# Grouping sixteen rounded and sixteen low matmuls in a Trainium2 encoder block, with aligned operands and later residual loads

## The chip, the cores and the metric

The kernel runs on one core of one Trainium2 chip. The core has a matrix engine (TensorE, in the profile PE for its matmuls and PEld for its weight loads), a vector engine (VectorE, DVE), a scalar engine (ScalarE, ACT), a general engine (GpSimd, POOL) and a synchronizing engine (SyncE, SP) that here issues nearly all transfers. The engines run at the same time, each through its own queue in order, and wait for one another by semaphores. The metric is the time of one execution in microseconds (us) of the device; less is better.

## The reference

One encoder layer on 256 tokens of width 2048, in float32:

```python
h = rms_norm(x, attn_norm[i])
proj = h @ w_in[i]
qa, ka, va, qb, kb, vb, ga, gb = jnp.split(proj, split_points, axis=-1)
ya = windowed_gqa(qa, ka, va, rel_bias_table, sink_a[i])
yb = dilated_attention(qb, kb, vb, rel_bias_table)
merged = jax.nn.sigmoid(ga) * (ya @ w_branch_a[i]) + jax.nn.sigmoid(gb) * (yb @ w_branch_b[i])
x = x + merged @ w_out[i]
hf = rms_norm(x, ffn_norm[i])
g = dwconv_centred(hf @ w_ffn_gate[i], conv_w[i], conv_b[i])
x = x + (jax.nn.gelu(g) * (hf @ w_ffn_up[i])) @ w_ffn_down[i]
gate_p = jax.nn.sigmoid(rms_norm(x, ple_norm[i]) @ w_ple_gate[i])
x = x + gate_p * (p[i] @ w_ple_proj[i])
return rms_norm(x, final_norm)
```

There are 8 heads of windowed attention and 12 of dilated attention in three groups, and the MLP is 5632 wide. Nearly all the time goes into the products with the weight matrices.

## The kernel before

**Rounded and low parts.** Products run in a rounded float format (FR in the code). To keep float32 accuracy each operand is split in two: a rounded part, made by ScalarE, and a low part, the rest, made by VectorE as the difference. Three products of parts make one product of the wanted accuracy: rounded by rounded, rounded by low and low by rounded.

**Weights.** All weights come from HBM as 258 pieces of 1 MB, in the order of their use. `load` (L238) has SyncE fetch a piece into one of three raw tiles. `produce` (L244) splits one unit, usually half a piece, 128 x 1024: ScalarE rounds it (L261, `uh`), VectorE takes the difference (L262, `ul`). There are six buffers for each of `uh` and `ul`, and two more of each, `vh` and `vl`, for units made of sums of weights (L254 to L256), in stages that save one product of eight by a Strassen-like scheme. `drop` (L279) gives a unit's buffers back and `pump` (L267) makes the next units at once, as far as buffers are free.

**Two kinds of stage.** In a feature-major stage the weights stand still in the array and the activations move: a block (`block`, L284) multiplies one 128 x 128 piece of weights by one 128-feature slice of the activations. Its first matmul (L289) takes the rounded weights and 512 columns, which are the 256 tokens' rounded and low parts side by side; its second (L290) takes the low weights and the rounded 256 columns, and adds to the second half of the same accumulator. `product` (L295) runs sixteen blocks for the 2048 features of one 128-wide result. The attention's queries and keys (activations `hs`) and the MLP's gate and up projections (activations `hf`) are made so: 544 and 1408 blocks. In the MLP's first half, stage E0, the first four products run jointly, feature slice by feature slice (L952 to L956); E1 is the second half. The first seven products of the attention run jointly too, in a loop of their own at the start (L517 to L529). In a token-major stage the activations stand still and 512 columns of weights move, in threes (`thirds`, L321, lines L324 to L326): gates, branch projections, output projection (D0 and D1), the MLP's way down (F00 to F11) and the last gate. Value products (L302, lines L312 to L314) are of that kind with 256 columns.

**What hangs between blocks.** Work on the side is put down by `at` for a stage, a feature slice and a place, and `run_due` runs it when the loop comes by: the scores of a head (L581 to L583 and L600) at slice 9 of the product after its query, the transposes of the exponentials (L635) at slice 11 or 12 of the next, the product with the values (again L581 to L583) at slice 4 of the one after that. At the MLP's start the last transposes of the activations (`rows_pair`, L812) are put down for slices 2 to 5. A scheduler then sets the final order on each engine, so that rows can move a little from where the code has them; `keep` (L400) pins an instruction to the program's order.

**Residual rows.** The input's rows, to which the output projection adds, are loaded in four transfers of 512 KB into `xr` (`load_rows`, L869), put down for pieces 3 to 6 of stage D0. `xr` takes the place of `ya`, the windowed attention's result, and can't land before its last reader is done.

**Memory.** Tiles stand in pools. Up to the pools of weights and of large activations every tile starts at 160 modulo 512 bytes. The pool `sc` of small tiles has an uneven size, and behind it the attention's tiles and later the token stages' tiles (`vh`, `vl`, sums of activations `S`, a third part of the MLP's activations `act2`) start at 352 modulo 512.

Of the kernel before, what the change touches and what calls it, by code (L numbers as in the profile page):

```python
# [10 lines left out]
F32 = mybir.dt.float32  # L11
# [5 lines left out]
P = 128  # L17
T = 256
D = 2048
KC = D // P  # L20
# [7 lines left out]
NH = QH + BH  # L28
# [57 lines left out]
START = FIRST + 1  # L86
WARM = 9
JOINT = 4
WIDE = 2 * T
_JOBS = _plan()  # L90
NA = len(_JOBS)
# [94 lines left out]
def _encoder(ctx: ExitStack, tc, xt, pt, xrow, cols, gainrow, table, onehot, mask, ident_in, wts, out):  # L186
# [97 lines left out]
    def block(acc, m, first, last):  # L284
# [7 lines left out]
        if o == _LAST_OF[u]:  # L292
            drop(u)

    def product(i, moving, n, ring):  # L295
        acc = bank(ring)
        for k in range(n):
            run_due(i, k)
            block(acc, moving(k), k == 0, k == n - 1)
        return acc  # L300

    def value_product(i, paired):  # L302
# [178 lines left out]
    hs = big.tile([P, KC, 2 * T], FR, name="hs", tag="R0")  # L481
    tot = ap_.tile([P, T], F32, name="tot", bufs=1)
    oh = ap_.tile([NBUCK, 2 * T], F32, name="oh", tag="near", bufs=1)
    tb = sc.tile([NBUCK, NH], F32, name="tb", bufs=1)
    mk = ap_.tile([NH, 2 * T], F32, name="mk", tag="s1", bufs=2)

    order = [(0, 1), (0, 0, 3), (0, 3, 7), (1, 2), (0, 7, 11), (0, 11, PIECE), (2, 3)]
    chunk = 3
# [96 lines left out]
    def scores(heads, y):  # L585

        n = len(heads)
        wide = T if n == 1 else 2 * T
        s = ap_.tile([P, 2, wide], F32, name="s", tag="s%d" % n, bufs=2 if n == 1 else 1)
        h, k = heads[0]  # L590
        sp = bank("sp", P, 2, T)
        for t in range(2):
            thrice(sp[:, t, :], [qs[h][:, c + t * P:c + (t + 1) * P] for c in (0, T)], [ks[k][:, :T], ks[k][:, T:]])
        a, step = (hba[:, h, :], P) if n == 1 else (hbb[:, h - QH, :], 1)
        nc.vector.tensor_tensor(s[:, :, :T], sp, view(a, 0, (step, 2), (1, T)), op=ALU.add)
        if n > 1:
            sp = bank("sp", P, 2, T)
            for g, (h, k) in enumerate(heads[1:]):
                for t in range(2):
                    nc.tensor.matmul(sp[:, t, g * P:(g + 1) * P], qs[h][:, t * P:(t + 1) * P],  # L600
                                     ks[k][:, (1 - t) * P:(2 - t) * P], start=True, stop=True)
# [12 lines left out]
        for t in range(2):  # L614
            nc.scalar.activation(s[:, t, :], s[:, t, :], AF.Exp, bias=nm[:, t:t + 1], accum_out=den[:, t:t + 1])
        if n == 1:
            es = ap_.tile([P, 2], F32, name="es")
            nc.scalar.activation(es, nm, AF.Exp, bias=sk)
            nc.vector.tensor_tensor(den, den, es, op=ALU.add)
        rd = ap_.tile([P, 2], F32, name="rd")  # L620
        nc.vector.reciprocal(rd, den)
        for t in range(2):
            nc.vector.tensor_scalar(s[:, t, :], s[:, t, :], rd[:, t:t + 1], None, op0=ALU.mult)
        return s
# [203 lines left out]
            at(when, merged_pair, "P22", 2 * j + i, c)  # L828

    def halved(r):  # L830
        h = sc.tile([P, 2], F32, name="rh")
        nc.vector.tensor_scalar(h, r[:, :2], 0.5, None, op0=ALU.mult)
        return h

# [32 lines left out]
    xr = big.tile([P, 2, D], F32, name="xr", tag="ya")  # L867

    def load_rows(n):  # L869
        nc.sync.dma_start(xr[:, :, cut[n]], xrow[:, :, cut[n]])  # L870

    def residual(stage, s, moving, key, square):

# [14 lines left out]
        turn_back(which, pair, dst, lambda t: xr[:, t, pair * T:(pair + 1) * T], scale)  # L888

    def rows_root():  # L890
        q = sc.tile([P, 2], F32, name="rs")
        nc.vector.tensor_tensor(q, held["ssq"][:, 0], held["ssq"][:, 1], op=ALU.add)
        return root(q, 2)

    for n in range(4):
        at(("D0", 3 + n, 0), load_rows, n)
    at(("D0", 2, 4), combine, "merged", held["merged"], 6, 2)
    held["ssq"] = sc.tile([P, 2, 2], F32, name="ssq")
    residual("D0", 0, lambda k: held["merged"][:, k, :], "merged", True)
    hf = big.tile([P, KC, 2 * T], FR, name="hf", tag="R0")  # L900
    for pair, when in enumerate((("D1", 0, 2), ("D1", 0, 5), ("D1", 1, 0), ("D1", 1, 3))):
# [43 lines left out]
    for half in range(2):  # L945
# [4 lines left out]
        joint = 0 if half else JOINT  # L950
        stage = "E%d" % half
        accs = [bank(which) for which in ("M1", "M5", "M6", "M7")[:joint]]  # L952
        for k in range(KC if joint else 0):
            run_due(stage, k)
            for a in accs:
                block(a, hf[:, k, :], k == 0, k == KC - 1)  # L956
        for (kind, n), a in zip(jobs, accs):
            mlp(kind, n, a)
        turns["e"] = 0
# [2 lines left out]
        if half:  # L962
# [6 lines left out]
            held["ssq"] = sc.tile([P, 2, 2], F32, name="ssq")  # L969
# [143 lines left out]
```

## Time and profile before

| | |
|---|---|
| median of 3 runs | 1474.07 us (1472.39 to 1474.58) |
| the profiled execution | 1474.83 us, of which the span of the trace is 1473.0 |
| granted TensorE clock | 0.998 |
| VectorE busy | 84% of the span |
| ScalarE busy | 55% of the span |
| moved by DMA | 282.93 MB, mean 192 GB/s |

The prediction shows the lines that carry it. A row of a group reads: line of the code, engine, operation, out<-in by the names of the tiles, shapes, count; then busy time in us and the mean of one in ns; then the engine's idle time before them and who ended it. Durations of matmuls include their way through the array and overlap with the next, so that the pace of a run of matmuls is the difference of two starts, divided by the number of steps between them. A row of the timeline begins with its start in us from the span's start and its duration.

### The profile page before, as it was taken

To read this page: it belongs to the slowest core of one execution; us is meant where nothing else is said; L and a number is where in the kernel's file an instruction comes from. 1 tells how busy PE (TensorE), PEld (TensorE's weight loads), DVE (VectorE), ACT (ScalarE), POOL (GpSimd) and SP (SyncE) were. 2 spreads that over 40 slices of the span, in tenths; PEclk is the share of its full clock that TensorE was granted. 3 is DMA by queue.
4 is the path that set the end of the run, shared out by engine and by line. 5 is a ranking of instruction groups with operands and counts; after the bars stand their busy time and mean duration, and the time that the engine had idled before them with its cause. 6 is when DMAs were issued, how large, how long until landed. Compare 5 with 4: busy or idle time off the path is not lost.

```text
span 1473.0 us, 20121 instructions
## 1 busy us (share of the span) xinstructions
PE 1456.9 (99%) x7766; PEld 1247.8 (85%) x7766; DVE 1241.5 (84%) x1841; ACT 810.5 (55%) x1153; POOL 4.8 (0%) x9
## 2 busy tenths in 40 slices
PE   9999999999999999999999999999999999999997
PEld 8899999988888887888888888888888888888785
DVE  7587665669989989989888899988888889999994
ACT  7466444446555555565555556454555555555763
POOL 0000000000000000000000000000000000000000
PEclk9999999999999999999999999999999999999999
DMA  9654454445456456464555545465545455446462
GB/s 318 236 199 144 154 184 178 160 155 200 172 200 229 169 211 248 155 234 185 199 183 189 201 152 219 181 248 176 196 176 196 178 194 179 184 188 232 168 222 93
DMA packets 46460, 282.93 MB, mean 192 GB/s; under 512 B 5076, under 2 KB 9812, under 8 KB 14108
## 3 DMA queue, kind: packets, MB, share of 16 engines
q1 hardware_dynamic: 45356, 280.20, 52.1%
q10 hardware_dynamic: 1008, 1.45, 0.3%
q8 instruction: 61, 1.00, 0.3%
q14 instruction: 35, 0.29, 0.1%
HBM read 279.49 MB, written 2.14 MB: 191 GB/s over the span
## 4 chain that ended last, share of the span: by engine, by line
PE 91%; DVE 4%; DMA 2%; ACT 1%; issue 1%; POOL 0%; POOLq 0%; ACTq 0%
PE bank L289 31%; PE bank L290 15%; PE bank L324 12%; PE bank L325 12%; PE bank L326 12%; DMA raw<-in_wts 2%; PE bank L312 2%; PE bank L313 2%; PE bank L314 2%; DVE ul L262 1%; DVE vl L262 1%; ACT uh L261 1%; PE bank L812 1%; PE bank L635 0%; PE bank L582 0%
## 5 line engine op out<-in xcount | busy, mean ns | idle before, releaser
L261 ACT ACTIVATE uh<-raw 128x1024 fp32r<-128x1024 f32 (+2 forms) x518 | 522.6, 1017 | 493.1 <-PE bank L289 272.0
L262 DVE TENSOR_TENSOR ul<-raw,uh 128x1024 fp32r<-128x1024 f32 (+2 forms) x518 | 601.0, 1171 | 184.4 <-ACT uh L261 181.8
L289 PE MATMUL bank<-hf,uh 128*128 128x512 f32 x1408 | 493.6, 397 | 0.0
L290 PE MATMUL bank<-hf,ul 128*128 128x256 f32 x1408 | 393.4, 280 | 0.0
L289 PEld LDWEIGHTS bank<-hf,uh 128*128 128x128 f32 x1408 | 264.6, 188 | 63.1
L290 PEld LDWEIGHTS bank<-hf,ul 128*128 128x128 f32 x1408 | 265.7, 189 | 0.2
L289 PE MATMUL bank<-hs,uh 128*128 128x512 f32 x544 | 195.9, 402 | 2.1 <-DVE hs L422 2.1
L290 PE MATMUL bank<-hs,ul 128*128 128x256 f32 x544 | 153.5, 283 | 0.0
L261 ACT ACTIVATE vh<-raw 128x1024 fp32r<-128x1024 f32 x92 | 97.4, 1058 | 59.9 <-DVE raw L254 28.3
L289 PEld LDWEIGHTS bank<-hs,uh 128*128 128x128 f32 x544 | 103.5, 190 | 25.0 <-DVE hs L422 2.4
L262 DVE TENSOR_TENSOR vl<-raw,vh 128x1024 fp32r<-128x1024 f32 x92 | 112.2, 1221 | 0.5 <-ACT vh L261 0.2
L290 PEld LDWEIGHTS bank<-hs,ul 128*128 128x128 f32 x544 | 104.3, 192 | 0.1
L324 PE MATMUL bank<-uh,act 128*128 128x512 f32 x232 | 90.8, 391 | 0.0
L325 PE MATMUL bank<-ul,act 128*128 128x512 f32 x232 | 90.7, 391 | 0.0
L326 PE MATMUL bank<-uh,act 128*128 128x512 f32 x232 | 90.7, 391 | 0.0
L324 PE MATMUL bank<-uh,hs 128*128 128x512 f32 x172 | 67.6, 393 | 0.0
L326 PE MATMUL bank<-uh,hs 128*128 128x512 f32 x172 | 67.5, 392 | 0.0
L325 PE MATMUL bank<-ul,hs 128*128 128x512 f32 x172 | 67.3, 391 | 0.0
L312 PE MATMUL bank<-uh,hs 128*128 128x256 f32 x224 | 63.8, 285 | 0.0
L313 PE MATMUL bank<-ul,hs 128*128 128x256 f32 x224 | 63.5, 283 | 0.0
L314 PE MATMUL bank<-uh,hs 128*128 128x256 f32 x224 | 63.4, 283 | 0.0
L254 DVE TENSOR_TENSOR raw<-raw 128x1024 f32<-128x1024 f32 x46 | 56.2, 1222 | 0.5
(236 smaller groups left out, 2232.4 us busy)
## 6 DMA issues: line engine op xcount, KB each, us to landing
raw<-in_wts SPq DMA_DIRECT2D x251, 1024.0 KB, 4.8
raw<-in_wts SPq DMA_DIRECT2D x12, 512.0 KB, 6.7
xr<-in_xrow SPq DMA_DIRECT2D x4, 512.0 KB, 9.8
x<-in_xt SPq DMA_DIRECT2D x13, 128.0 KB, 5.8
hb<-hold SPq DMA_DIRECT2D x3, 514.0 KB, 7.6
hb<-hold SPq DMA_DIRECT2D x2, 768.0 KB, 6.6
last<-in_gainrow SPq DMA_DIRECT2D x1, 1024.0 KB, 4.8
out<-xr SPq DMA_DIRECT2D x4, 256.0 KB, 2.6
```

Of the source, the lines that this page charges most:

```text
L254: nc.vector.tensor_tensor(raw[:, :2 * WIDE], raw[:, WIDE:3 * WIDE], raw[:, :2 * WIDE], op=ALU.subtract)
L261: nc.scalar.activation(hi, src, AF.Copy)
L262: nc.vector.tensor_tensor(lo, src, hi.bitcast(F32), op=ALU.subtract)
L289: nc.tensor.matmul(acc, hi[:, w], m, start=first, stop=False, skip_group_check=True)
L290: nc.tensor.matmul(acc[:, T:], lo[:, w], m[:, :T], start=False, stop=last, skip_group_check=True)
L312: nc.tensor.matmul(acc[:, :T], xh, hi, start=(k == 0), stop=False)
L313: nc.tensor.matmul(acc[:, :T], xh, lo, start=False, stop=False)
L314: nc.tensor.matmul(acc[:, :T], xl, hi, start=False, stop=(k == KC - 1))
L324: nc.tensor.matmul(acc, sh, wh, start=first, stop=False)
L325: nc.tensor.matmul(acc, sh, wl, start=False, stop=False)
L326: nc.tensor.matmul(acc, sl, wh, start=False, stop=last)
L812: nc.tensor.transpose(p[:, k, t * P:(t + 1) * P], src(t)[:, k * P:(k + 1) * P], ident)
```

## The change

Three edits, and what they move.

**Grouping.** `products` and `unit_blocks` take the place of the loops over `block` in `product` and in E0's joint part. Two units, sixteen blocks, are taken together: first the sixteen matmuls with rounded weights, and then the sixteen with low weights. Work that is due between blocks runs while the rounded matmuls are written out. Both units are given back during the low ones. The joint loop of the first seven products still uses `block`.

**Addresses.** `tb` moves from `sc` to the attention's pool, in the ring of the keys; `rh`, `rs` and `ssq` get one buffer each; the reciprocal's tile `rd` becomes 32 columns wide, of which two are used. By this the attention's tiles and the token stages' `vh`, `vl`, `S` and `act2` start at 160 modulo 512 bytes.

**Residual rows.** `load_rows` is pinned to the program's order.

```diff
+JOINED = 2
...
+    def unit_blocks(todo):
+
+        ends, units = [], []
+        for _ in range(JOINED):
+            u = _FBLOCKS[state["at"] + len(ends)][0]
+            units.append(u)
+            for o in range(_LAST_OF[u] + 1):
+                acc, m, first, last = next(todo)
+                nc.tensor.matmul(acc, weights(u)[0][:, o * P:(o + 1) * P], m,
+                                 start=first, stop=False, skip_group_check=True)
+                ends.append((acc, m, last, u, o))
+        for acc, m, last, u, o in ends:
+            nc.tensor.matmul(acc[:, T:], weights(u)[1][:, o * P:(o + 1) * P], m[:, :T],
+                             start=False, stop=last, skip_group_check=True)
+            if o == _LAST_OF[u]:
+                drop(u)
+        state["at"] += len(ends)
+
+    def products(i, moving, n, accs):
+
+        def todo():
+            for k in range(n):
+                run_due(i, k)
+                for acc in accs:
+                    yield acc, moving(k), k == 0, k == n - 1
+
+        blocks, end = todo(), state["at"] + n * len(accs)
+        while state["at"] < end:
+            unit_blocks(blocks)
...
     def product(i, moving, n, ring):
         acc = bank(ring)
-        for k in range(n):
-            run_due(i, k)
-            block(acc, moving(k), k == 0, k == n - 1)
+        products(i, moving, n, [acc])
         return acc
...
-    tb = sc.tile([NBUCK, NH], F32, name="tb", bufs=1)
+    tb = ap_.tile([NBUCK, NH], F32, name="tb", tag="k", bufs=7)
...
-        rd = ap_.tile([P, 2], F32, name="rd")
-        nc.vector.reciprocal(rd, den)
+        rd = ap_.tile([P, 32], F32, name="rd")
+        nc.vector.reciprocal(rd[:, :2], den)
...
-        h = sc.tile([P, 2], F32, name="rh")
+        h = sc.tile([P, 2], F32, name="rh", bufs=1)
...
-        nc.sync.dma_start(xr[:, :, cut[n]], xrow[:, :, cut[n]])
+        keep(nc.sync.dma_start(xr[:, :, cut[n]], xrow[:, :, cut[n]]))
...
-        for k in range(KC if joint else 0):
-            run_due(stage, k)
-            for a in accs:
-                block(a, hf[:, k, :], k == 0, k == KC - 1)
+        if joint:
+            products(stage, lambda k: hf[:, k, :], KC, accs)
```

On TensorE, in the product that holds the sums of squares for the first norm (`tot` by `ones`) and the spread of its root (`rdg`), blocks alternated before:

```order
L290 MATMUL bank<-hs,ul 128x256
L289 MATMUL bank<-hs,uh 128x512
L290 MATMUL bank<-hs,ul 128x256
L429 MATMUL bank<-ones,tot 128x1 x4
L289 MATMUL bank<-hs,uh 128x512
L290 MATMUL bank<-hs,ul 128x256
```

Now the same product and the first score matmul (`kf` by `qf`) of the next stand so:

```order
L304 MATMUL bank<-hs,uh 128x512 x6
L459 MATMUL bank<-ones,tot 128x1 x4
L304 MATMUL bank<-hs,uh 128x512 x8
L480 MATMUL bank<-rdg,ones 128x256
L304 MATMUL bank<-hs,uh 128x512 x2
L308 MATMUL bank<-hs,ul 128x256 x16
L304 MATMUL bank<-hs,uh 128x512 x9
L611 MATMUL bank<-kf,qf 128x256
```

The sixteen low matmuls have moved behind all rounded ones, and side work has only rounded matmuls of its own product ahead of it. In the MLP 86 of the 88 rounded groups stand as one row of sixteen.

On VectorE, around the last query (`q`) of a group of dilated heads and the eviction of its scores (`s`), before:

```order
L262 TENSOR_TENSOR ul<-raw,uh 128x1024
L411 SCALAR_TENSOR_TENSOR u<-bank,t 128x256
L659 TENSOR_TENSOR ya<-bank,ya 128x256
L712 TENSOR_TENSOR q<-u,rms 128x128x2
L262 TENSOR_TENSOR ul<-raw,uh 128x1024 x2
L411 SCALAR_TENSOR_TENSOR u<-bank,t 128x256
L712 TENSOR_TENSOR q<-u,rms 128x128x2
L262 TENSOR_TENSOR ul<-raw,uh 128x1024
L595 TENSOR_TENSOR s<-bank,hb 128x2x256
```

and now:

```order
L263 TENSOR_TENSOR ul<-raw,uh 128x1024 x2
L441 SCALAR_TENSOR_TENSOR u<-bank,t 128x256
L742 TENSOR_TENSOR q<-u,rms 128x128x2
L689 TENSOR_TENSOR ya<-bank,ya 128x256
L263 TENSOR_TENSOR ul<-raw,uh 128x1024 x2
L441 SCALAR_TENSOR_TENSOR u<-bank,t 128x256
L742 TENSOR_TENSOR q<-u,rms 128x128x2
L625 TENSOR_TENSOR s<-bank,hb 128x2x256
```

The low units now come in twos between the products' evictions, and the unit that stood between the query and the scores' eviction is among those ahead of the query.

On SyncE, around the loads of the residual rows (`xr`), before:

```order
L241 DMA raw<-in_wts 128x2048 x78
L870 DMA xr<-in_xrow 128x2x512 x2
L241 DMA raw<-in_wts 128x2048 x2
L870 DMA xr<-in_xrow 128x2x512 x2
L241 DMA raw<-in_wts 128x2048 x143
```

and now:

```order
L242 DMA raw<-in_wts 128x2048 x83
L900 DMA xr<-in_xrow 128x2x512
L242 DMA raw<-in_wts 128x2048
L900 DMA xr<-in_xrow 128x2x512
L242 DMA raw<-in_wts 128x2048
L900 DMA xr<-in_xrow 128x2x512
L242 DMA raw<-in_wts 128x2048
L900 DMA xr<-in_xrow 128x2x512
L242 DMA raw<-in_wts 128x2048 x137
```

The first load stands five raw tiles later than before, and one raw tile stands between each two of the four.

More of the change, by code (lines that the diff above doesn't have):

```diff
@@ L293, in block @@
             drop(u)
+    def unit_blocks(todo):
[23 more added lines that the diff above has]
+            unit_blocks(blocks)
+        assert next(blocks, None) is None
     def product(i, moving, n, ring):
         acc = bank(ring)
-        for k in range(n):
-            run_due(i, k)
-            block(acc, moving(k), k == 0, k == n - 1)
+        products(i, moving, n, [acc])
         return acc
@@ L890, in rows_root @@
     def rows_root():
-        q = sc.tile([P, 2], F32, name="rs")
+        q = sc.tile([P, 2], F32, name="rs", bufs=1)
         nc.vector.tensor_tensor(q, held["ssq"][:, 0], held["ssq"][:, 1], op=ALU.add)
@@ L897, in _encoder @@
     at(("D0", 2, 4), combine, "merged", held["merged"], 6, 2)
-    held["ssq"] = sc.tile([P, 2, 2], F32, name="ssq")
+    held["ssq"] = sc.tile([P, 2, 2], F32, name="ssq", bufs=1)
     residual("D0", 0, lambda k: held["merged"][:, k, :], "merged", True)
@@ L968, in _encoder @@
                 nc.vector.tensor_tensor(pl_[k], pr[:, k], ph_[k].bitcast(F32), op=ALU.subtract)
-            held["ssq"] = sc.tile([P, 2, 2], F32, name="ssq")
+            held["ssq"] = sc.tile([P, 2, 2], F32, name="ssq", bufs=1)
         residual("F%d0" % half, 0, activation_row, "act", half)
```

## The prediction

> **What bounds the kernel now.** I read the busy shares first, then the groups of instructions, the engine's own waits, and last the timeline of single matmuls, because the first view alone says only "TensorE".
>
> ```profile
> span 1473.0 us, 20121 instructions
> PE 1456.9 (99%) x7766; PEld 1247.8 (85%) x7766; DVE 1241.5 (84%) x1841; ACT 810.5 (55%) x1153; POOL 4.8 (0%) x9
> PE 91%; DVE 4%; DMA 2%; ACT 1%; issue 1%; POOL 0%; POOLq 0%; ACTq 0%
> ...
> PE bank L582 <- DVE qf L417: 0.7, 1, 0.7
> ```
>
> TensorE is busy for 99% of the span, it carries 91% of the chain that ended last, and its own list of waits, of which one is shown, holds six entries, none above 2.1 us. So nothing but the pace of the matmuls, and those few waits, can move the time much. Busy time doesn't tell the pace, since matmuls overlap: it has to be taken from start to start. The timeline of TensorE gives it (columns: start, duration, engine, line, operation). In the first half of the MLP, then in its second half:
>
> ```profile
> 699.85 0.28 PE L290 MATMUL bank<-hf,ul 128*128 128x256 f32 x1
> ...
> 710.94 0.28 PE L290 MATMUL bank<-hf,ul 128*128 128x256 f32 x1
> ```
>
> ```profile
> 1050.03 0.28 PE L290 MATMUL bank<-hf,ul 128*128 128x256 f32 x1
> ...
> 1060.99 0.28 PE L290 MATMUL bank<-hf,ul 128*128 128x256 f32 x1
> ```
>
> The first pair of rows spans 32 blocks (a block is one L289 and one L290): 11.09 / 32 = 346.6 ns each. The second spans 31: 10.96 / 31 = 353.5 ns. Nothing waits in either stretch; the same alternation simply settles into a fast or a slow beat. Two places show what a run of equal matmuls takes:
>
> ```profile
> 479.62 0.39 PE L325 MATMUL bank<-ul,ya 128*128 128x512 f32 x1
> ...
> 487.78 0.39 PE L325 MATMUL bank<-ul,yb 128*128 128x512 f32 x1
> ```
>
> ```profile
> 923.64 0.39 PE L326 MATMUL bank<-uh,act 128*128 128x512 f32 x1
> ...
> 936.88 0.39 PE L324 MATMUL bank<-uh,act 128*128 128x512 f32 x1
> ```
>
> ```profile
> 50.78 0.28 PE L314 MATMUL bank<-uh,hs 128*128 128x256 f32 x1
> ...
> 57.98 0.28 PE L314 MATMUL bank<-uh,hs 128*128 128x256 f32 x1
> ```
>
> 512 columns after 512 columns: 8.16 / 36 = 226.7 ns in the branch projections, and 13.24 / 58 = 228.3 ns in the down projection, where VectorE and ScalarE work harder. 256 after 256, in a value product: 7.20 / 60 = 120.0 ns. A rounded and a low matmul, each among its like, would thus take 346.7 to 348.3 ns: the fast beat, and never the slow one.
>
> **The change part by part.** The sum is made against the profiled execution, 1474.83 us (a span of 1473.0 and 1.8 around it), which is 0.76 above the median of 1474.07.
>
> *Grouping.* No instruction is added or removed; of 1952 blocks the 112 of the start stay alternating, and 1840 are grouped: 704 in each half of the MLP and 432 in the attention projections. I take 347.5 ns, the middle of 346.7 and 348.3. The second half gains 704 x (353.5 - 347.5) = 4.2 us, the first loses 704 x 0.9 = 0.6. For the attention projections the trace has this stretch and these means:
>
> ```profile
> 187.80 0.28 PE L290 MATMUL bank<-hs,ul 128*128 128x256 f32 x1
> ...
> 196.98 0.28 PE L290 MATMUL bank<-hs,ul 128*128 128x256 f32 x1
> ```
>
> ```profile
> L289 PE MATMUL bank<-hs,uh 128*128 128x512 f32 x526 | 187.1, 398 | 0.0
> L290 PE MATMUL bank<-hs,ul 128*128 128x256 f32 x528 | 147.9, 281 | 0.0
> L289 PE MATMUL bank<-hf,uh 128*128 128x512 f32 x1408 | 493.6, 397 | 0.0
> L290 PE MATMUL bank<-hf,ul 128*128 128x256 f32 x1408 | 393.4, 280 | 0.0
> ```
>
> 9.18 / 26 = 353.1 ns, the slow beat. The MLP's means of 397 and 280 ns come from one half fast and one slow; those of the attention projections are 1 ns higher each, so I put two thirds of their blocks in the slow beat: 288 x 5.6 - 144 x 0.9 = 1.5 us. Together -5.1 us; -6.5 at 346.7 ns and -3.6 at 348.3.
>
> By the Trainium skill, "TensorE: Matmul & The Clock Gate", section "Back-to-back issue gap", a warm matmul of N columns follows its predecessor after N / 2.4 + 2.5 ns, which is 215.8 and 109.2 here and 325 for a block in whatever order. The trace doesn't agree (346.6 and 353.5, against 226.7 and 120.0 in runs), and it is the difference between the orders that the term above uses.
>
> *What the grouping moves.* Six pairs of weight buffers feed TensorE. Two are now in hand at once, and the next pair of units is wanted two groups later, 2 x 16 x 0.3475 = 11.1 us, while making a unit takes this:
>
> ```profile
> L262 DVE TENSOR_TENSOR ul<-raw,uh 128x1024 fp32r<-128x1024 f32 x468 | 568.0, 1222 | 166.9 <-ACT uh L261 164.4 <-PE bank L289 1.6
> ```
>
> 2 x 1.22 = 2.4 us of VectorE, behind ScalarE's 1.06 each (the first row below): hidden. But work that hangs between blocks is reached sooner, since only rounded matmuls stand before it: at the tenth block by 9 x 125 ns = 1.1 us. The tightest such place is the score matmul that follows the last query of a head group:
>
> ```profile
> 152.36 1.06 ACT L261 ACTIVATE uh<-raw 128x1024 fp32r<-128x1024 f32 x1 [1.71 <-PE bank L289]
> 153.46 1.23 DVE L262 TENSOR_TENSOR ul<-raw,uh 128x1024 fp32r<-128x1024 f32 x1 [1.55 <-ACT uh L261]
> 155.05 0.64 DVE L712 TENSOR_TENSOR q<-u,rms 128x256 f32<-128x256 f32 x1
> 156.11 1.05 PE L600 MATMUL bank<-k,q 128*128 128x128 f32 x8
> ```
>
> The query is ready at 155.69, TensorE wants it at 156.11. TensorE arrives 1.1 us earlier, but the query does too, by about 1 us: ScalarE waited here for the product's last rounded matmul, which now stands 16 x 0.12 = 1.9 us before the product's end, so the rounded weights are made before the eviction instead of ahead of it. VectorE then makes two low units before the query, as the order shows. Two of the four such places lie in grouped products; with the chain at the first head (the 0.7 us wait above) and the transposes that start the MLP I allow +0.5 us, between 0 and 3 x 1.1 = 3.3.
>
> *Residual rows.* SyncE issued two of these loads at 545.03, behind a wait for the last reader of their buffer, and ahead of two raw tiles:
>
> ```profile
> 545.03 1.31 SPq L870 DMA_DIRECT2D xr<-in_xrow  x2
> 547.96 1.47 SPq L241 DMA_DIRECT2D raw<-in_wts  x2
> 547.96 7.46 DMA raw<-in_wts
> raw<-in_wts SPq DMA_DIRECT2D x251, 1024.0 KB, 4.8
> 555.52 1.06 ACT L261 ACTIVATE uh<-raw 128x1024 fp32r<-128x1024 f32 x1 [3.92 <-DMA raw<-in_wts]
> 558.76 0.39 PE L325 MATMUL bank<-ul,merged 128*128 128x512 f32 x1
> 560.83 0.66 PE L812 MATMUL bank<-ident,c 128*128 128x128 f32 x4 [1.69 <-DVE merged L816]
> ```
>
> The raw tile took 7.46 us where the median is 4.8, ScalarE stood for it, VectorE's queue slid, and TensorE lost 2.07 - 0.23 = 1.84 us at the transposes. Issued at the same 547.96 and landing in 4.8 it would be there 2.7 us sooner, more than the stall: -1.8 us (bounds 0 and -1.8). What is late next? The first load now goes five raw tiles later, some 5 x 4.8 = 24 us, near 569; with the median landing of 9.8 us it is there at 579, and its reader starts at 594:
>
> ```profile
> xr<-in_xrow SPq DMA_DIRECT2D x4, 512.0 KB, 9.8
> L878 DVE TENSOR_TENSOR xr<-xr,bank x4: 678/683/687, 594.3 to 600.2; 128x512 f32<-128x512 f32 x4
> ```
>
> *Residues.* The pools move, so that the token-stage tiles lose their offset of 352 and stand at 160 modulo 512, as the others do. Where operands of both kinds meet, matmuls are a little longer:
>
> ```profile
> L324 PE MATMUL bank<-uh,act 128*128 128x512 f32 x232 | 90.8, 391 | 0.0
> L324 PE MATMUL bank<-uh,S 128*128 128x512 f32 x46 | 18.3, 399 | 0.0
> L325 PE MATMUL bank<-ul,S 128*128 128x512 f32 x46 | 18.2, 396 | 0.0
> L326 PE MATMUL bank<-uh,S 128*128 128x512 f32 x46 | 18.1, 393 | 0.0
> L325 PE MATMUL bank<-vl,act 128*128 128x512 f32 x20 | 8.0, 401 | 0.0
> L324 PE MATMUL bank<-vh,S 128*128 128x512 f32 x138 | 54.5, 400 | 0.0
> ```
>
> Against 391: 46 x (8 + 5 + 2) = 0.7 us, and some 60 matmuls at 10 ns, 0.6. The 138 at 400 have both operands at 352 and wait for VectorE at times; at 9 ns they hold 1.2 more. Bounds 0 and -2.5; I take -1.5, near the 1.3 of the mixed rows. The other edits (single buffers, a wider reciprocal tile) move addresses alone and cost nothing.
>
> By the Trainium skill, "SBUF — State Buffer", section "Who interferes with whom", "PE and ACT never wait on anyone", so addresses should not matter. The rows of 399 and 401 ns lean the other way, though they differ in more than the residue.
>
> **Sum.** -5.1 - 1.8 - 1.5 + 0.5 = -7.9 us: 1466.9 for the profiled execution, and **1466.2** beside the median of 1474.07.
>
> **Rivals.** *Residues give nothing* (the rows differ because of waits): 1467.7. That is also the time by the SBUF page's rule.
>
> *The slow beat survives grouping*, or the order doesn't matter: for it speaks that the same code holds both beats, against it that no long run of equal matmuls shows the slow one. Without the first term: 1471.3. The TensorE page's formula would give this too.
>
> *Early arrival ends slower.* Twelve heads have scores and transposes between blocks, and four transposes start the MLP. If TensorE waits the full 1.1 us at each of 16 places, that costs 17.6, less 8.4 saved: 1483.3. It turns the sign from the eighth place on. Against it: one wait of 0.7 us is all that TensorE's list shows there today.
>
> *The change doesn't do what it says*: the scheduler could split the groups. The order shows 86 of the MLP's 88 rounded groups whole, so no chance of its own.
>
> **How the numbers follow.** The forecast 0.42, residues nothing 0.25, slow beat 0.18, early arrival 0.08, better than every bound 0.07. With all bounds at their best the sum is -10.8, which is 1463.3; with all at their worst -0.3, 1473.8. The range 1462.0 to 1473.8 takes in the first three cases and leaves out most of the last two, 0.15. A change of 0.2%, 2.9 us, is about what a measurement of this kernel can tell from none: faster (below 1471.1) 0.42 + 0.25 + 0.07 and a third of the slow-beat case, less 0.02 for a forecast with its terms at their worst, 0.78; within it 0.14; slower 0.08.
>
> **What would show it.** Start to start, 512-column matmuls of the second half at 226.7 to 228.3 ns and 256-column ones at 120; both halves of the MLP equally long; no wait before L812 near 560; the rows of S at 391. Wrong would be: rounded groups above 233 ns, new waits of TensorE for q, s or xr, a first reader of the residual rows that waits for a DMA.

## The result and the profile after

| | before | after |
|---|---|---|
| median of 6 runs each | 1473.09 us | 1466.06 us (1464.90 to 1467.14) |
| ratio, 95% interval | | 0.9951 (0.9938 to 0.9963) |
| the profiled execution, and its span | 1474.83 us, 1473.0 | 1467.14 us, 1465.3 |

The time is 0.14 us from the forecast of 1466.2. This is partly luck. The forecast started from 1474.07 us; beside the change the kernel before took 1473.09, so by the medians the gain is 7.0 us where 7.9 were forecast. And the profile shows two terms that were wrong by almost 2 us each, in opposite directions.

Busy shares and the chain that ended last, from the page of the kernel after:

```profile
span 1465.3 us, 20083 instructions
...
PE 1450.7 (99%) x7766; PEld 1250.4 (85%) x7766; DVE 1248.0 (85%) x1841; ACT 826.2 (56%) x1153; POOL 4.9 (0%) x9
...
PE 97%; DVE 1%; DMA 1%; ACT 1%; issue 1%; POOLq 0%; POOL 0%; ACTq 0%
```

TensorE carries 97% of the chain, 91% before. TensorE's own waits after (waiter, who ended it: total us, times, longest):

```profile
PE bank L290 <- DVE hs L452: 1.8, 1, 1.8
PE bank L355 <- DVE vl L263: 1.1, 2, 0.8
PE bank L224 <- DVE mhalf L219: 1.1, 1, 1.1
PE bank L354 <- ACT last L1035: 0.4, 1, 0.4
PE bank L354 <- ACT vh L262: 0.3, 1, 0.3
```

The 1.7 us for `merged` is gone, and none of the feared waits for `q`, `s` or `xr` is there. New at the start of F1 is the wait of L355 and L354 for the low and rounded sums `vl` and `vh`; before, a single wait for `vl`, of 0.4 us, stood in the last gate. TensorE's timeline in the middle of E1, the MLP's second half (x16: a run of sixteen in one row; the last row is cut off by the end of the window):

```profile
1050.02 3.82 PE L304 MATMUL bank<-hf,uh 128*128 128x512 f32 x16
1053.67 2.08 PE L308 MATMUL bank<-hf,ul 128*128 128x256 f32 x16
1055.58 3.82 PE L304 MATMUL bank<-hf,uh 128*128 128x512 f32 x16
1059.23 2.08 PE L308 MATMUL bank<-hf,ul 128*128 128x256 f32 x16
1061.15 1.09 PE L304 MATMUL bank<-hf,uh 128*128 128x512 f32 x4
```

From 1050.02 to 1061.15 stand 32 blocks: 347.8 ns each, where it was 353.5. A rounded group takes 3.65 / 16 = 228.1 ns a matmul, a low one 1.91 / 16 = 119.4.

Since the ends of matmuls overlap, the stages are best measured from the start of their first matmul to the start of the next stage's first. Lengths in us, worked out so from the traces of before, of after, and of seven of the experiments below ("queries" is the attention from its first value product to the first gate; B0 to B3 are the gates alone; E0 and E1 are the MLP's halves, F0 and F1 their ways down):

| stage | before | e2 keep | e3 addresses | e1 grouping | after | e4 at 352 | e5 late split | e11 alternating | e12 rdg |
|---|---|---|---|---|---|---|---|---|---|
| queries | 261.69 | 261.78 | 262.01 | 260.47 | 260.53 | 260.47 | 260.52 | 260.53 | 261.91 |
| B0 to B3 | 173.22 | 173.25 | 172.18 | 173.18 | 172.16 | 173.32 | 172.15 | 172.17 | 172.17 |
| D0, D1 | 88.14 | 86.25 | 87.56 | 87.95 | 85.81 | 86.29 | 85.77 | 85.77 | 87.03 |
| E0 | 246.32 | 246.35 | 250.71 | 247.30 | 247.29 | 247.28 | 247.29 | 250.71 | 246.34 |
| F0 | 113.84 | 113.85 | 112.91 | 113.83 | 112.95 | 113.86 | 112.96 | 112.91 | 113.01 |
| E1 | 248.73 | 248.73 | 248.73 | 244.90 | 244.90 | 244.90 | 244.91 | 248.73 | 248.73 |
| F1 | 116.20 | 116.21 | 115.50 | 119.17 | 117.77 | 118.46 | 115.51 | 115.59 | 115.76 |

The columns of before and after already show the gain in E1 and D0, a little in each token-major stage, a loss in E0, and one of 1.57 us in F1, which nothing in the prediction speaks of.

### The profile page after: what moved, and what is told of

Same layout as the page of the kernel before. It is cut to its first block, busy times and chain, and to the rows that moved or that the text cites. A ratio compares the mean times of both kernels' runs of the same rounds, so it can differ in the third digit from the quotient of the medians.

```text
span 1465.3 us, 20083 instructions
## 1 busy us (share of the span) xinstructions
PE 1450.7 (99%) x7766; PEld 1250.4 (85%) x7766; DVE 1248.0 (85%) x1841; ACT 826.2 (56%) x1153; POOL 4.9 (0%) x9
## 4 chain that ended last, share of the span: by engine, by line
PE 97%; DVE 1%; DMA 1%; ACT 1%; issue 1%; POOLq 0%; POOL 0%; ACTq 0%
PE bank L304 29%; PE bank L308 15%; PE bank L354 14%; PE bank L355 14%; PE bank L356 14%; PE bank L290 2%; PE bank L342 2%; PE bank L343 2%; PE bank L344 2%; PE bank L291 1%; PE bank L842 1%; PE bank L665 0%; DMA pair<-in_pt 0%; PE bank L612 0%; PE bank L613 0%
## 5 line engine op out<-in xcount | busy, mean ns | idle before, releaser
L304 PE MATMUL bank<-hf,uh 128*128 128x512 f32 x1408 | 336.5, 391 | 0.0
L304 PEld LDWEIGHTS bank<-hf,uh 128*128 128x128 f32 x1408 | 258.6, 188 | 50.1
L308 PEld LDWEIGHTS bank<-hf,ul 128*128 128x128 f32 x1408 | 180.7, 191 | 6.9
L308 PE MATMUL bank<-hf,ul 128*128 128x256 f32 x1408 | 183.0, 283 | 0.0
L304 PE MATMUL bank<-hs,uh 128*128 128x512 f32 x432 | 109.7, 395 | 0.0
L435 ACT ACTIVATE t<-bank 128x256 f32<-128x256 f32 x122 | 46.5, 384 | 81.9 <-PE bank L308 71.8
L354 PE MATMUL bank<-uh,act 128*128 128x512 f32 x232 | 90.4, 390 | 0.0
L355 PE MATMUL bank<-ul,act 128*128 128x512 f32 x232 | 90.4, 390 | 0.0
L304 PEld LDWEIGHTS bank<-hs,uh 128*128 128x128 f32 x432 | 77.5, 189 | 13.5
L354 PE MATMUL bank<-uh,hs 128*128 128x512 f32 x172 | 67.3, 391 | 0.0
L355 PE MATMUL bank<-ul,hs 128*128 128x512 f32 x172 | 67.2, 390 | 0.0
L308 PEld LDWEIGHTS bank<-hs,ul 128*128 128x128 f32 x432 | 55.4, 191 | 2.2
```

The costliest lines, as they stand in the source:

```text
L304: nc.tensor.matmul(acc, weights(u)[0][:, o * P:(o + 1) * P], m, start=first, stop=False, skip_group_check=True)
L308: nc.tensor.matmul(acc[:, T:], weights(u)[1][:, o * P:(o + 1) * P], m[:, :T], start=False, stop=last, skip_group_check=True)
L354: nc.tensor.matmul(acc, sh, wh, start=first, stop=False)
L355: nc.tensor.matmul(acc, sh, wl, start=False, stop=False)
L435: keep(nc.scalar.activation(t, acc[:, T:], AF.Copy, scale=scale))
```

## The experiments

All times are medians, each beside runs of the kernel before. The ratios are those on record; they are made from all runs and can differ from the quotient of the two medians by 0.05%.

| run | us | before beside it | ratio, 95% interval |
|---|---|---|---|
| e1 grouping alone | 1471.06 | 1472.62 | 0.9994 (0.9986 to 1.0003) |
| e2 pinned loads alone | 1471.11 | 1472.62 | 0.9995 (0.9986 to 1.0004) |
| e3 addresses alone | 1473.90 | 1472.62 | 1.0006 (0.9998 to 1.0015) |
| e4 after, tiles back at 352 | 1469.28 | 1472.62 | 0.9976 (0.9967 to 0.9985) |
| e5 after, p split late | 1463.97 | 1473.65 | 0.9932 (0.9920 to 0.9945) |
| e6 after, groups of two | 1465.27 | 1473.65 | 0.9944 (0.9931 to 0.9958) |
| e7 after, groups of eight | 1466.49 | 1473.65 | 0.9953 (0.9940 to 0.9965) |
| e8 before again | 1472.98 | single run | |
| e9 addresses alone again | 1475.13 | single run | |
| e10 MLP alternating, with a lead-in | 1470.88 | 1472.81 | 0.9986 (0.9977 to 0.9995) |
| e11 MLP alternating | 1471.15 | 1472.81 | 0.9990 (0.9981 to 0.9999) |
| e12 addresses alone, rdg back | 1469.23 | 1472.94 | 0.9977 (0.9968 to 0.9986) |

### The three edits one by one

**e1, grouping alone.** The kernel after without the address edits and without `keep`.

```diff
-        keep(nc.sync.dma_start(xr[:, :, cut[n]], xrow[:, :, cut[n]]))
+        nc.sync.dma_start(xr[:, :, cut[n]], xrow[:, :, cut[n]])
...
-    tb = ap_.tile([NBUCK, NH], F32, name="tb", tag="k", bufs=7)
+    tb = sc.tile([NBUCK, NH], F32, name="tb", bufs=1)
```

> Only the grouping is taken over; addresses and residual loads stay as before. Theory (the grouping removes the slow beat, each edit's gain is its own): 512-column matmuls of the MLP at 228.5 ns and 256-column ones at 119.5 ns as in the changed kernel, E1 shorter by 3.8 us, E0 longer by 1.0, the attention shorter by 1.2, the stall near 560 still there; 4 to 5 us less than before (ratio 0.997). Rival (the edits only gain together, because mixed residues would slow the grouped matmuls too): E1 gains less than 2 us and the whole less than 2 us.

The ratio of 0.9994 can't be told from no change. The stages say why: E1 gains 3.83 us and the queries 1.22, E0 loses 0.98, together -4.07, inside the bounds of the grouping's term; but F1 gives 2.97 us back. The grouping does what it should, and something behind it eats most of it. The forecast of 4 to 5 us less missed for that reason.

**e2, pinned loads alone.** The kernel before with one line of the change.

```diff
-        nc.sync.dma_start(xr[:, :, cut[n]], xrow[:, :, cut[n]])
+        keep(nc.sync.dma_start(xr[:, :, cut[n]], xrow[:, :, cut[n]]))
```

> Only the residual loads are pinned behind the raw tiles. Theory (they delayed one raw tile and so the transposes at the start of D0): the 2 us gap before the transposes in D0 is gone, D0 shorter by 1.8 us, nothing else changes, 1.8 us less than before (ratio 0.9988). Rival (the stall is VectorE's and comes back a little later): a gap of over 1 us elsewhere in D0, D0 shorter by less than 0.6 us.

TensorE's timeline of this kernel at the transposes that had waited:

```profile
558.01 0.40 PE L325 MATMUL bank<-ul,merged 128*128 128x512 f32 x1
558.24 0.60 PE L812 MATMUL bank<-ident,c 128*128 128x128 f32 x4
558.60 0.48 PE L326 MATMUL bank<-uh,merged 128*128 128x512 f32 x1
```

The transposes follow their predecessor after 0.23 us instead of 2.07. D0 and D1 lose 1.89 us and no other stage moves by more than 0.1. As a share of the whole that is 0.13%; the interval of the ratio takes in no change as well, so it is the trace that shows it.

**e3, addresses alone.** The kernel before with the edits of `tb`, `rd`, `rh`, `rs` and `ssq`.

> Only the addresses change. Theory (mixed residues lengthen 512-column matmuls by 5 to 10 ns): the rows of S with uh fall from 399, 396 and 393 to 391 ns, the gates B0 to B3 shorter by 1.1 us together, the whole 1.5 to 2 us less (ratio 0.999). Rival (the rows differ because of waits, addresses don't matter): the rows stay at 393 to 399 and the time is the same within 0.5 us.

There is no gain in the whole, yet the token-major stages are shorter: B0 to B3 by 1.04 us, D by 0.58, F0 by 0.93, F1 by 0.70, together 3.25. E0 takes it back: 250.71 instead of 246.32 us. It now runs in the slow beat, with nothing in its code changed.

TensorE at the end of F0, where `act2` stands in the array, before (it lies at 352 modulo 512):

```profile
994.92 0.39 PE L326 MATMUL bank<-uh,act 128*128 128x512 f32 x1
...
998.35 0.39 PE L326 MATMUL bank<-uh,act 128*128 128x512 f32 x1
```

and with the address edits alone (at 160):

```profile
996.41 0.39 PE L326 MATMUL bank<-uh,act 128*128 128x512 f32 x1
...
999.81 0.39 PE L326 MATMUL bank<-uh,act 128*128 128x512 f32 x1
```

Both pairs of rows span fifteen steps: 3.43 / 15 = 228.7 ns before, 3.40 / 15 = 226.7 now. The printed durations are 0.39 in both.

**e4, the kernel after with its tiles back at 352.** One tile of `sc` is made 192 bytes wider, which moves all pools behind it; the order of instructions is that of after.

```diff
-    known = sc.tile([P, 2], F32, name="known", bufs=1)
+    known = sc.tile([P, 50], F32, name="known", bufs=1)[:, :2]
```

> The changed kernel with one tile of the small pool made 192 bytes larger, so that the attention's and token stages' tiles stand at 352 modulo 512 again; every engine's order of instructions is that of the changed kernel. Theory (the residue itself costs): the rows of S with uh are back at 393 to 399 ns and the time is 1.5 to 2 us above the changed kernel (ratio to before 0.9963). Rival (the order that came with the address edits, not the residue): rows at 391 ns and the time of the changed kernel (0.9951).

The time goes up from a ratio of 0.9951 to 0.9976. Against after, B0 to B3 are 1.16 us longer, D 0.48, F0 0.91, F1 0.69: 3.24 us, in the same stages and to the same size as e3 from the other side. E0 and E1 don't move: grouped, they aren't sensitive to these addresses. The spans of the two profiled executions don't show the loss, 1465.4 us against 1465.3, because in e4's the first seven products took 40.1 us and in that of after 43.3; that stretch differs from trace to trace of one kernel too (42.7 and 41.7 in the two of before), so the stages and the medians have to be compared.

### The loss in F1

At F1's start in the kernel after, on ScalarE and VectorE (ACTq is ScalarE's transfer queue):

```profile
1238.37 0.33 ACTq L992 DMA_DIRECT2D pair<-in_pt  x1
...
1244.62 0.72 ACT L995 ACTIVATE t<-pair 128x256 fp32r<-128x256 f32 x2 [2.93 <-DMA pair<-in_pt]
```

```profile
1245.07 0.42 DVE L996 TENSOR_TENSOR u<-pair,t 128x256 fp32r<-128x256 f32 x1 [2.78 <-ACT t L995]
```

and on TensorE:

```profile
1250.89 0.50 PE L355 MATMUL bank<-vl,S 128*128 128x512 f32 x1 [0.32 <-DVE vl L263]
...
1252.65 0.50 PE L354 MATMUL bank<-vh,S 128*128 128x512 f32 x1 [0.31 <-ACT vh L262]
...
1253.91 0.50 PE L355 MATMUL bank<-vl,S 128*128 128x512 f32 x1 [0.76 <-DVE vl L263]
```

In the kernel before the same two instructions of ScalarE were:

```profile
1244.57 0.34 ACTq L964 DMA_DIRECT2D pair<-in_pt  x1
...
1249.27 0.42 ACT L967 ACTIVATE t<-pair 128x256 fp32r<-128x256 f32 x1
```

The issues of this transfer, with KB and us to the landing, before and after:

```profile
pair<-in_pt ACTq DMA_DIRECT2D x1, 256.0 KB, 4.6
```

```profile
pair<-in_pt ACTq DMA_DIRECT2D x1, 256.0 KB, 6.2
```

The rounding of `p` (L995, L967 before) stands in ScalarE's queue ahead of the units for F1. Before, it came 4.70 us after its transfer was issued and found the data there. Now ScalarE reaches it at 1241.69, 3.3 us after the issue, and stands there 2.93 us. So about half of the stand comes from reaching the work sooner, and the other half from the transfer, which itself takes 1.6 us longer; why it does, no run tests. VectorE, whose next instruction needs `t`, stands for 2.78, and the sums of weights `vh` and `vl` come late by what is left of it. From start to start the five steps of TensorE around its three waits are 2.2 us longer than five of 227 ns.

**e5, the kernel after with the split of p put down later.** `p` is wanted only at the very end, so its rounding and difference are put down for a place in F1.

```diff
-            for k in range(2):
-                nc.scalar.activation(ph_[k], pr[:, k], AF.Copy)
-                nc.vector.tensor_tensor(pl_[k], pr[:, k], ph_[k].bitcast(F32), op=ALU.subtract)
+            def split():
+                for k in range(2):
+                    nc.scalar.activation(ph_[k], pr[:, k], AF.Copy)
+                    nc.vector.tensor_tensor(pl_[k], pr[:, k], ph_[k].bitcast(F32), op=ALU.subtract)
+
+            at(("F10", 3, 0), split)
```

> The changed kernel, with the split of the per-layer embedding's input p moved from the end of E1 to the fourth piece of F10. In the changed kernel ScalarE stood 2.9 us and VectorE 2.8 us for the transfer of p at the end of E1, and TensorE then lost about 2 us in the first pieces of F1. Theory (those 2 us are the transfer's, reached earlier because E1 is shorter): no idle time of ScalarE for p, F1 shorter by 1.5 to 2 us, the whole 1.5 to 2 us below the changed kernel (ratio to before 0.9938). Rival (VectorE is full there and F1's first sums are late anyway): the stall stays within 0.5 us, time as the changed kernel (0.9951).

On ScalarE and VectorE of this kernel:

```profile
1243.63 0.73 ACT L997 ACTIVATE t<-pair 128x256 fp32r<-128x256 f32 x2 [3.08 <-DMA pair<-in_pt]
...
1253.21 0.42 DVE L998 TENSOR_TENSOR u<-pair,t 128x256 fp32r<-128x256 f32 x1
```

F1 falls from 117.77 to 115.51 us, as short as with the addresses alone, and no other stage moves; the waits for `vl` and `vh` are gone. ScalarE still stands 3.08 us for the transfer, since the scheduler put the rounding as early as it could. VectorE no longer does: its part comes ten microseconds later. The expectation of no idle time on ScalarE missed, and for that the run tells more: it was VectorE's stand that cost TensorE the time, and the price of the stall is 2.26 us. This is the best kernel of the study, 0.9932 against 0.9951 for the change; the two were not run side by side, but in the stages of the table their traces differ in F1 alone.

### The size of a group

**e6, groups of two blocks**, and **e7, groups of eight**. `unit_blocks` counts blocks instead of units:

```diff
-        for _ in range(JOINED):
-            u = _FBLOCKS[state["at"] + len(ends)][0]
...
+        for i in range(2):
+            u, o = _FBLOCKS[state["at"] + i]
```

> The changed kernel with groups of two blocks: two rounded matmuls, then two low ones. Theory (each matmul costs its columns plus a constant 13 ns for changing the weights, and only the strict alternation of 512 and 256 columns falls into the slow beat): a block of the MLP at 346.7 to 348.3 ns in both halves, time within 1 us of the changed kernel (0.9951). Rival (every change between 512 and 256 columns can cost, so half as many changes save half): E1 at about 350 ns, 1 to 2 us gained instead of 5.

> The changed kernel with groups of eight blocks, one unit each. Theory (constant cost, slow beat only in alternation): as the changed kernel, 0.9951 within 0.0007. Rival (buffers handed back in twos cost or gain something): the time moves by over 1.5 us against the changed kernel, and ScalarE's waits for L304 change with it.

Two blocks give 245.22 us in E1, eight 245.79, sixteen 244.90: 348.3, 349.1 and 347.9 ns a block. So neither "longer is better" nor "any grouping" is right. TensorE with groups of eight:

```profile
1050.70 2.00 PE L303 MATMUL bank<-hf,uh 128*128 128x512 f32 x8
1052.54 1.12 PE L307 MATMUL bank<-hf,ul 128*128 128x256 f32 x8
1053.50 2.00 PE L303 MATMUL bank<-hf,uh 128*128 128x512 f32 x8
```

Eight rounded take 1.84 us, 230 ns each, against 228.1 in sixteen; eight low 0.96, 120 each. The start of a rounded run is what costs. By place in the group, over the 44 groups of E1 in the kernel after, the first five rounded matmuls are 233, 236, 228, 232 and 231 ns from their successors and all later ones 226.7; the first two low ones 113 and 119, and all later ones 120.0. That is 27 - 8 = 19 ns a group above its steady pace: 1.2 ns a block in sixteen, 2.4 in eight. 346.7 plus that is 347.9 and 349.1, as measured in E1. Groups of two are in a pattern of their own. What the 13 ns of e6's theory go for, no run shows. In both kernels F1 takes 115.51 us: the split finds `p` landed (its ScalarE waits 0.3 us with groups of two, not at all with eight). That is why e6 comes out at 0.9944 although its halves of the MLP are 1.06 us longer than after. And that e7, at 0.9953, comes out where its theory had it is luck: its halves are 2.64 us longer (1.75 of it in E0, which the start of the runs explains by half), and F1 is 2.26 us shorter.

### The beat of the alternating kernels

e3 left a question: why does E0 fall into the slow beat when only addresses change?

**e8 and e9, the kernel before and the addresses alone, once more**, with no edit.

> The kernel of before once more, for the beat of its two MLP halves. In the first profile the halves had 231.8 + 115.0 and 236.7 + 116.6 ns from start to start. Theory A (the beat belongs to the code and its addresses): 346.7 ns a block in the first half and 353.3 in the second again, so 246.3 and 248.7 us. Theory B (each execution falls into a beat anew at the start of a stage): the first half can come out at 250.7 us, or the second at 244 to 245. An equal pair alone doesn't decide; it counts together with the next run.

> The kernel with the address edits alone once more. Its first profile had the slow beat in both halves (250.7 and 248.7 us). Theory A (the beat belongs to the code and its addresses): the same again. Theory B (each execution falls into a beat anew): the first half can come out at 246.3 us.

E0 took 246.34 us in e8 and 250.71 in e9, E1 248.73 in both: each kernel its first lengths again. The second traces speak for theory A, that the beat comes with the kernel, and nothing in them for theory B.

**e10 and e11, the late split with the MLP alternating**, with and without one group of sixteen at the start of each half.

```diff
-            unit_blocks(blocks)
+            unit_blocks(blocks, 1 if str(i).startswith("E") else 16)
```

> The late split of p, attention grouped by sixteen as after the change, and in each half of the MLP one group of sixteen as a lead-in with every other block alternating. If the matmuls ahead of a stretch of alternation set its beat, both halves have the same one, since both now follow sixteen low matmuls: either 346.7 ns a block, E0 near 246.3 and E1 near 244.1 us and the whole 1.8 us below the late split alone (ratio near 0.992), or 353.3 ns, E0 near 250.9 and E1 near 248.7 and 7.4 us above it (ratio near 0.998). If the beat comes by chance, the halves may differ.

> The late split of p, attention grouped by sixteen, the MLP alternating from its first block as before the change. If what stands ahead sets the beat, E0 and E1 come out as in the runs without grouping: E1 slow at 248.7 us, E0 at 246.3 or 250.7; so 2.9 to 7.3 us above the late split with everything grouped (ratio 0.995 to 0.998). If grouping the MLP had brought nothing in itself, it would be as fast as the late split alone (0.9932).

In their traces, without a lead-in E0 takes 250.71 and E1 248.73 us, with it 250.66 and 248.63: the slow beat in all four stages. Against e5 the alternating MLP costs 3.42 + 3.82 = 7.24 us. So on the new addresses the grouping of the MLP is worth more than twice its worth on the old ones (2.85 us in e1). The lead-in itself changes nothing. In E1, which nothing breaks into, sixteen low matmuls ahead don't turn the beat. In E0 it had no chance to, since transposes and other matmuls stand between the first blocks, and the beat that lasts starts behind the last of them. Timeline of TensorE with the addresses alone (e3's first profile), E0:

```profile
652.11 0.39 PE L289 MATMUL bank<-hf,uh 128*128 128x512 f32 x1
...
653.15 0.39 PE L289 MATMUL bank<-hf,uh 128*128 128x512 f32 x1
...
653.50 0.59 PE L450 MATMUL bank<-rdg,ones 128*128 128x256 f32 x2
...
696.68 0.40 PE L289 MATMUL bank<-hf,uh 128*128 128x512 f32 x1
...
699.86 0.40 PE L289 MATMUL bank<-hf,uh 128*128 128x512 f32 x1
```

Ahead of L450 three blocks take 1.04 us, 346.7 ns each: the fast beat. Behind it nine take 3.18, 353.3 each, to the end of the stage. In the kernel before the fast beat goes on behind the same matmul (the prediction's first pair of rows). Block by block, the slow beat is a cycle of three: in E1 of the kernel before, most blocks take 349, 350 and 361 ns in turn, so the loss of 20 ns sits in every third block. The fast beat has two forms with the same mean: even blocks of 347 ns, or 350 and 344 in turn. L450 multiplies `ones` by `rdg`, a small tile of the norm that lies at 448 modulo 512 before and at 352 with the address edits.

**e12, the addresses alone with rdg back at 448.** `rdg` is given 96 bytes ahead of its data, and small tiles behind it are arranged so that all other operands of TensorE keep e3's addresses, except those of sixteen matmuls at the very end.

```diff
-        dg = sc.tile([P, T], F32, name="rdg", bufs=1)
+        dg = sc.tile([P, T + 24], F32, name="rdg", bufs=1)[:, 24:]
...
-    known = sc.tile([P, 2], F32, name="known", bufs=1)
+    known = sc.tile([P, 10], F32, name="known", bufs=1)[:, :2]
...
-        v = sc.tile([P, 1], F32, name="v3")
+        v = sc.tile([P, 1], F32, name="v3", tag="rv")
...
-        r = sc.tile([P, 1], F32, name="r3")
+        r = sc.tile([P, 1], F32, name="r3", tag="rr", bufs=4)
```

> The address edits alone (e3_addr_only, in both profiles E0 250.7 us, span 1472.6 and 1473.3), with one thing put back: the operand rdg of the last matmul that breaks into E0's alternation (and rms and u behind it) stands at 448 modulo 512 again, as before the change, and every other operand that TensorE reads stays where the address edits put it. In the traces the beat of E0 changes at this very matmul: ahead of it all kernels without grouping run alike, behind it 346.7 ns a block with rdg at 448 and 353.3 with rdg at 352. If what happens at that matmul sets the beat of the stage: E0 246.3 us, E1 slow at 248.7 as ever, B to F short as in the first profile of the edits, the whole 4.4 us below them, ratio near 0.9976. If the beat hangs on the addresses of the attention and token tiles: E0 250.7 us and a ratio near 1.0006.

TensorE in E0 of this kernel:

```profile
652.22 0.59 PE L450 MATMUL bank<-rdg,ones 128*128 128x256 f32 x2
...
696.68 0.39 PE L289 MATMUL bank<-hf,uh 128*128 128x512 f32 x1
...
699.80 0.39 PE L289 MATMUL bank<-hf,uh 128*128 128x512 f32 x1
```

Nine blocks take 3.12 us, 346.7 ns each: the fast beat is back, E0 takes 246.34 us, and the ratio is 0.9977 where 0.9976 was expected. Eight traces have an alternating MLP: with `rdg` at 448 (before, e2, e8, e12) E0 is fast, with it at 352 (e3, e9, e10, e11) slow. Shown is that moving this tile, with `rms` and `u` behind it, turns E0's beat; only these two places were tried. What happens inside TensorE at that matmul is not shown, nor why E1, which no such matmul breaks into, is slow in all eight.

## Why the prediction was right, and where it was not

From the profiled execution of before to that of after the span fell by 7.7 us; 7.9 were forecast. By the stages and the runs that isolate them:

| term | forecast | measured | from |
|---|---|---|---|
| grouping, its own stages | -5.1 (-6.5 to -3.6) | -4.0 | E1 -3.83, E0 +0.97, queries -1.16 |
| early arrival, moved work | +0.5 (0 to 3.3) | +2.3 | F1, after against e5 |
| residual rows | -1.8 | -1.9 | D0, e2 |
| residues | -1.5 (-2.5 to 0) | -3.2 | B, D, F, e3 and e4 |
| start and end | none | -0.6 | first seven products +0.62, after F1 -1.24 |

They add up to -7.4 of the -7.7. The last row is mostly not the change's: the start took 40.1 to 43.3 us in the fourteen traces, and the last gate, 85.47 us in the first trace of before, took 84.82 in its second and 84.6 to 84.8 in all others, with the change or without.

**The bound and the beat** were right. TensorE's pace is the time, runs of equal matmuls don't show the slow beat, and both halves of the MLP now run at one pace: E1 takes 347.9 ns a block, inside the 346.7 to 348.3 forecast; E0 is longer by its transposes. The term came out smaller by 1.1 us, in good part since each rounded run starts with five slow matmuls, which the stretches behind the estimate, inside long runs, didn't hold. That 347.5 ns came so near 347.9 is luck. Its upper end rests on the 228.3 ns of the down projection, which the prediction put down to busier VectorE and ScalarE. It was the residue: the same 58 steps, which hold matmuls of `S`, `vh` and `vl`, take 226.7 ns each in e3, where only the addresses differ. The two thirds of the attention's blocks in the slow beat were about right: 381 of them that nothing interrupts have a mean of 350.8 ns before. The Trainium skill, "TensorE: Matmul & The Clock Gate", section "Back-to-back issue gap", has a formula for the gap of a single warm matmul, by which 215.8 and 109.2 ns would be the estimates here; the trace has 226.7 and 120.0 in long runs, and the order of the two widths moves a block between 346.7 and 353.3.

**Early arrival** failed in its place. The prediction looked at the scores, the transposes and the first head, and none of them waits. The work that was reached too soon was the rounding of `p`, which hangs on a transfer and stands ahead of F1's first units on two engines: +2.3 us. About half of the stand behind it is the longer transfer, 6.2 us where it took 4.6, of which the prediction had nothing. The term lies inside its bounds by luck, since they were made for other places. The rival "early arrival ends slower" came true at one place, which is none of its sixteen.

**Residual rows** were right in place and size. The first load is now issued at 568.9 us (569 was forecast) and the first reader of the rows doesn't wait.

```profile
L900 SPq DMA_DIRECT2D xr<-in_xrow x4: 550/553/669, 568.9 to 579.7; - x4
```

That row is the line's own answer in the kernel after (min, median and max of the issues in ns, first and last start).

**Residues** were mis-sized, -1.5 forecast and -3.2 measured. The step that failed is "against 391": the prediction priced mean durations, right after it had said that durations don't tell the pace. Rows with `S` did fall to 391 as forecast:

```profile
L354 PE MATMUL bank<-uh,S 128*128 128x512 f32 x46 | 18.0, 391 | 0.0
```

But the time is in the steps from start to start. Before and e3 run the same matmuls in the same order, so the steps of the threes can be compared one by one (those over 260 ns in either left out):

| operand at 352 before | steps | before, ns | e3, ns | together, us |
|---|---|---|---|---|
| the standing one | 231 | 230.9 | 227.3 | 0.83 |
| the moving one | 136 | 233.7 | 227.5 | 0.85 |
| both | 397 | 229.0 | 227.6 | 0.53 |
| neither | 1969 | 227.8 | 227.1 | 1.35 |

The prediction had 1.3 us for the first two rows and nothing for the last; 1.1 of its 1.35 us lie within six matmuls of one that has such an operand. The four sums aren't exactly the 3.2 us of the stages, since they leave out the long steps and take in the last gate. The kernel after and e4 give the same four sums to 0.1 us. The Trainium skill, "SBUF — State Buffer", section "Who interferes with whom", says that PE never waits on anyone. That section speaks of ports that engines share and not of addresses; that "addresses should not matter" was the prediction's own conclusion, and e4, which changes addresses alone and costs 3.24 us, refutes it. What in the chip makes the difference, no run shows.

**What the sum could not hold** is that the terms depend on each other. On their own, the edits are worth 0.06%, 0.05% and -0.06% by the ratios of the table, none of them clear of no change, and 0.49% together. The addresses alone lose 4.4 us in E0 by the beat, and the grouping takes that sensitivity away; e5 against e11 puts it at 7.2 us in the MLP. The prediction compared with the beats of before, which was right for the change as a whole, and would have been wrong for the addresses by themselves.

## What to carry to other kernels

Where one engine is busy for 99% of the span, measure its pace from start to start in every stage, and compare stage lengths before totals: three edits that each measured as nothing were here worth 0.5% together, and the reasons stood in the stages. When work is reordered, look first for instructions that hang on a transfer and stand in the queue ahead of the stage that follows; here one of them could be put later, and no other stage moved. In this kernel equal matmuls kept one pace in runs, past the first five; the alternation fell into a slower beat, which in E0 the address of one small matmul's operand decided.

## What the runs showed of the hardware that was not expected

- Alternating 512- and 256-column matmuls hold one of two mean paces, 346.7 or 353.3 ns a pair, through the 660 undisturbed pairs of E0 and the 704 of E1; the slower is a cycle of three pairs of 349, 350 and 361 ns. Moving one operand of 1 KB a partition by 96 bytes (with two small tiles behind it) changed it in E0, and the second traces of two kernels kept it.
- The change from 256 to 512 columns and back costs some 19 ns in groups of eight and sixteen: five rounded matmuls at 228 to 236 ns before the pace settles at 226.7, less 8 ns in the first two low ones.
- 512-column matmuls whose operands lie at 352 and 160 modulo 512 bytes, or both at 352, took 1 to 6 ns more from start to start than with both at 160, and matmuls near them took more too; over B, D and F that made 3.2 us, while the durations hardly showed it.
